# First row tiles transposed before they are scaled, the first scale made in one piece, and a new order, in a decoder layer kernel

## The chip, the core and the metric

The kernel runs on one core of a Trainium2 chip. A core has a matrix engine (TensorE, PE in the profile; its weight loads are shown as PEld), VectorE (DVE), ScalarE (ACT), GpSimd (POOL) and a sync engine (SP) whose queue issues all DMAs here. Matrix products read SBUF and write PSUM, which has 8 banks of 128 x 512 float32. The metric is the device time of one execution in microseconds (us), the median of several runs.

## The reference

One layer, sequence 1024, width 1024, float32. Only the first steps matter here:

```
mod = silu(c) @ w_mod + b_mod            # w_mod: 1024 x 6144; c: one vector
sh1, sc1, g1, sh2, sc2, g2 = split(mod)  # six vectors of 1024
h    = rms_norm(x, norm_mix_w) * (1 + sc1) + sh1
proj = h @ w_in                          # key, z, query, value, lru columns, beta and alpha
```

After that come a gated linear recurrence and a chunked gated delta rule (with a triangular inverse for each chunk), an output projection, a squared-ReLU MLP and a last norm.

## The kernel before

**Products.** A float32 operand is split into two fp32r parts, a high one (`hh`, `wkh`) and a low one (`hl`, `wkl`), and a product is made of three: high by high, high by low, low by high (`mm3`). Transposes, sums and the products for `mod` are plain float32, which the profile records twice for each product.

**Order.** `Recorder` collects every operation of all engines; `schedule` then places them, engine by engine, by a priority, with estimated durations, and `emit` writes them out in that order (line 475 issues them all, so nearly every row of the profile says L475). The priority of an operation is its place in the code at the start (`rec.early`) and its latest start later, plus a number of its own from the table `SHIFTS`. Some operations of PE are only fillers: `WARM` products of a tile of ones with itself (tile `warm`), taken when no other operation of PE is ready in the plan. Once written out, each engine keeps its order: a filler then takes its time whether PE has to wait or not.

**The start** (lines 675 to 1027). The tokens of x are eight row tiles `x0` to `x7`, 128 x 1024. `xnorm(t)` makes the sum of squares on ACT (tile `xj`), its power -1/2 on POOL (`rs`) and scales the tile. Then 128 x 128 blocks are transposed on PE into PSUM, multiplied there by the column `A1 = (1 + sc1) * norm_mix_w` and split: `hh` on ACT, `hl` on DVE. `sh1` is brought in as two extra columns of `h`.

- `scale1(q)` makes `A1` in three pieces (256, 256 and 512 columns of `sc1`). For the first two, PE multiplies `cact` = silu(c) by the weights (`sc_r`, a row of 256 sums in 8 products), DVE copies the row, and one-column products turn it into columns (`sc_c`). For the third, ACT and DVE sum weights times `cact` (`sc_acc`), and 8 one-column products add up the partitions.
- `xquarter` transposes and scales blocks of two row tiles, `xhalf` of four.
- `Key.first` makes the first key products, of the first 512 tokens, four heads of one PSUM bank each (`k_p`): of the first two blocks of `h` in two halves of 256 tokens, of the others in 512. `splitk` splits the key weights `wk`.
- `Key.second` follows with tokens 512 to 767 and the rest; between them stand `ab_third` (tile `ab`, the beta and alpha columns) and the sum for `sh1` (`sh_acc` on ACT and DVE, `sh_c` on PE). The z, query, value and lru projections, the delta rule and the MLP come later.

Of the kernel before, what the change touches and what calls it, by code (L numbers as in the profile page):

```python
# [47 lines left out]
FILL, WARM, AB_DUR, GATE_DUR, L1_DUR, L2_DUR = 1e6, 36, 0.85, 0.89, 0.07, 0.14  # L48
# [7 lines left out]
TABLE = 1.28  # L56
RESERVE = {"b": 11, "ps": 2, "u": 1, "c": 2}
# [67 lines left out]
def dram_box(ap):  # L125
# [7 lines left out]
    'c-p;NXLuFWy8hOhGzcXW30?5es~}a1VCWn`L7Ef+QBXiQqI8rhND~wk2pttfX;OtylwL!ZlF%U}p``8X?Cd@Bo_FWo`{zE-?0Y9a&g99HWY2uF*80l(z'  # L133
    '3-YyCKjQ)H9^YC<D}|VGGY*hW-70qr9Q?AX(@e>h5af*8-~|Y5>aZ0yoxJ0i^cduPN6rpSjBNAd5(1Om6!GE4E{o$gxKWg(p;|MU+VDvb&nP&hCi8+I4'
    'dC`VMEfv<dnpSq$<ycJe&0Fz_ZiO!jmgKpOD(*MWQDnWld_(^PL!tbZa-#5*OgrjMlPIl&na7fFjZi^HPgIq_~=c9x7P&$j%otpYN9TvI&y$)$>v>3d#'
    'JGo*8A8q;1Xm*8Lgh-YP8}ZJ&l3h0Q*4@Yy)5loQ_bXfJ1y`r;EzHFl`8>U_$NdTja}1j!z(OFxRu8I!DrX@BzXhVrT9OMOL-b3`kBq0!y<Fyk+ELYiZ'
    '4dMXxLv&Bk}aCMTl8RKzW*6WTijYxc_%gaFhvV`c-@~%E_EXG5te8~5rCBMYT6x7r{Y>}gBgRLw?>p4;+E7&zjX2=JU*E3(@T=%jfbb_qYC4!IZSlvdh'
    '>*=oh+N<sw_q12W>G-TmYKqZJCAoh!$E)S~JAFPYQbypR>XLa(^_K~{WM*}>N%qTM))tIa^JQ&zL1VV(Mp`Picvj0i>1oB|v@ubwbAPLPsiaKHx`SO<f'
    '~l$r(yWTI$2=k(u@&#*4Yfg@$p{&Oe|kn(ORN;sw6^=2WDSr3^0sQC;*EUfY}}IZ@~u9rPDy9!oHbR>Tj#8GnJ&b5cDdiMhGUF(G}@!OF9^H6OY~(aVH'
    'TB|yzc^u&AQ-u-71HNo<5nCWEryYz{*HXw>D#MW(mo{H@M`Q>;8w^>wZ78k^7*T<=Sk$>rJsztj=-=argi~BHoo`)pk{P|B!jl)j8u$w0FOf9iQFSo#N'  # L140
    '{0nw3$*HxP|7j$3D}1J*-tQ1<Z5f$sCJWA5J=|J(9X=16Y?v%jxy<_bJE_gS?vg0RXe>e}I1ZbryVRPwC#b;9?IO+NK&)}+iw@M0Kdm{&2&{23LkerA~'
    '3z_o2c9+XG_tc%{7mO_53s%xh8n)^NTmgjF@InP9IPtPUa6f@c<4v#P3)Z(J!F=8E$(ae<p@G-=k%6R=>R~ZuIb6YXKj#3XROw+rGsNupYl*SHxY!;Js'
    '%$IVq9{bG8Xz#5k$FqY`-Z~4*J=whC9_vfa{L<aabJcuib;BBtR>x;B-$zIV&tB9=g6CHD)a*}vkyb0SKk`~9d>-F+^Fwp5S;3o$3BIn<TDti9Nk!Q!h'
    'kQ}8Nv39>_KwTCf&JNyef1FR>F-_Zo0)YweYCrSd#k&QtB$L6dfklf=`)dld?;+D`6^2ntDr=Bx?>VDnQINaKYPMa$!zK?ZFaRjl=*nqcf<VMS`5vcoG'
    '5LinVd7Xn)S@r%=?Zb{|(|X6!&n;w*jl<CSJg0mXbPFvQ-)FkZKLZal}~@Es=-F%UUceXAolr5h<pj2?qE+!{1oVue);2id2TYC10~DM_3oo6#Kb?z39'
    '(*j<5z`Ju$Gg<2(Z`dP^z_%VCaPTxv)e*&rq^V>9+)CARaoCAf<G@&XY=>q-)-6LFd-@~L#x*Ht&2f^)b)q<KwJtcohX8j9)C%!tx0f{tKIP?_MH##E!'
    'RJmNhHvs*cxpBB?BgW6ECMB4H1lknkJ`BI`d*9;8c+=t3Xk|0%;KRHY2^Lm&Lmt^AB7L}@Is~}xpO34Wr%EV1;vw9|dq?_)m8mJ|BfQ9O?{Hb>;7kZ(B'
    ')RT*hb_sbRk1<6JQ%`j<Jx*;=f66G;S-$dj7I`E)6r`NQt2?M6qok9RmJcPbZlvz0@oEe^<tepC-J+j9(@W)`)|}^JW36m4MoV>Lw!W;B*l$DCdexY0V'
    '6|GH_Nz9sOA0Yl=HNB?fqt&VDr?Glwv}gaqbnm)i;MeMmr-T)MD>eYL9h|b>)M7?mpLjuXr$4`NKuFMSfi=D926CDP-co{G*C|^Lw4#x#zpBC{EM0?(R'
    '!tERi4W+sbG8}Kk7>Ck}LFVwNR((TPjSKlZL^IBsOTU5h;DygHz$pi*WfyF00#8ovVC?ZTL~9NfIVXwA|!pZ%Q25LSH#76J(_>B|D4~avjr*`sxie&)6'  # L150
    'bfBP=LH#mG@9p`z3>M2c6>!&hpW+)&HaTzNyF2FVR1qphrAt++8n*X6p0%XV3<pX!Y|EGR)&Qe}-As=EG3n(8m4r!18}SP9kSEblW?&d~SEINJ^?PU`d'
    'LVzMpg_@^9Oggdr4fv24JY_cY&$7ANF)1#_m3kwa&FE*lsW6L1r+<)a9TXc|Ygc1MhIksHMY;k(zacr>^Q`l47%)T;2t_TU@x7*M5C7rQP=g&o~Y(<p4'
    'B2!gIc9xMcpP!VGNGamjfqPkfA3L7oImZ@_WCyO{37LIw)Req(3nj$^iyb0S!iZI^abJ8qUqK3!U*5wja*-bBgM#uAqS@18_}44+e^d^FJ3Er_7VVrKB'
    '^+CHlWW*1UD#9h61!_-ri?^!nZ-{^N&y+piVc(P`YzTHmx3i95q7<*s(gr+cd0oRT3(!l+bS#f(NsQ_R#+nk(Nrx*sPs`w*}LM%k<K#%Dv~X|qG}swuv'
    'PM-H7hO=<<u=>z4eY<)T{L_j8nDsr|Os$rK-tyYLFU6wiC)O@&tl6;lV}bmm+%3RcR`kv+AqQsdK6hXA#UkQQ7gzhcUj+Yxh;h7T~O>;UiT@%1d?i4l^'
    'bXz50#3Pgb-_g|jP$>9V?uYN2;Zf378u^x%riNH%?NLA6vPrL;QC?w`r;&Ft8#c+WBX{)4kmQXyjKJW^LLkT<m(?bQ(~>U1QtpRSPY2+kEFUMA%nJI1*'
# [72 lines left out]
class Recorder:  # L229
# [64 lines left out]
    def schedule(self):  # L294
# [40 lines left out]
        while done < len(ops):  # L335
# [115 lines left out]
            for j in op.succs:  # L451
# [4 lines left out]
                if kind and o.eng == "PE" and not o.bb:  # L456
                    r += SLACK_TINY if o.tiny and op.eng == "DVE" else SLACK
# [128 lines left out]
def hybrid_body(ctx, tc, x, c, norm_mix_w, norm_mlp_w, w_mod, b_mod, w_in,  # L586
# [202 lines left out]
    for a in range(4):  # L789
        load_sc1(2, a)  # L790
# [188 lines left out]
    for k in (2, 3):  # L979
        xhalf(0, k)  # L980
# [942 lines left out]
```

## Time and profile before

| | |
|---|---|
| median of 3 runs | 1150.64 us (1147.06 to 1154.63) |
| profiled execution: its time | 1149.7 us |
| its span, first to last instruction | 1147.8 us |
| PE busy | 1135.8 us of it |
| mean granted clock of PE | 0.996 |
| first key product starts | 20.89 us |
| first `ab` product starts | 75.67 us |

The profile was taken on one execution. Rows of a timeline give start, length, engine, operation, the tile written and the tiles read, and how often the operation follows itself; in brackets stands how long the engine was idle before, and what ended that. PE's rows overlap, since a product's end lies behind the start of the next; what one takes of PE is read from start to start. The clock of PE is 1.00 or 0.50 at any moment; a value between is a mean over a stretch.

### The profile page before, as it was taken

The page shows a single profiled execution, that of the slowest core. Times are in us where ns is not written, and L with a number is a line of the kernel's source. Part 1 is how long each engine was busy: PE and PEld are TensorE (multiplying, and loading weights), DVE is VectorE, ACT ScalarE, POOL GpSimd, SP SyncE. Part 2 cuts the span into 40 slices and gives each one's busy share as a digit, 9 for nine tenths or more (in the row PEclk, how much of TensorE's full clock was granted, in tenths as well). Part 3 has the DMA queues.
Part 4 walks back from the last instruction along what each step waited for, and adds up shares of the span by engine and source line. Part 5 has one row for each costly group of instructions (what it writes and reads, how often), then busy time and mean ns, then how long its engine had stood idle before and what let it go on. Part 6 is the DMA issues. An engine that isn't in the chain of part 4 may idle for free.

```text
span 1147.8 us, 16549 instructions
## 1 busy us (share of the span) xinstructions
PE 1135.8 (99%) x6288; PEld 971.7 (85%) x6288; DVE 823.0 (72%) x1143; ACT 611.0 (53%) x961; POOL 274.8 (24%) x161
## 2 busy tenths in 40 slices
PE   8999999999999999999999999999999999999997
PEld 5889998999999987888888888887888888888886
DVE  3559898688888869679767677576874485774673
ACT  4535815454567895577645454556744343452362
POOL 1101100021211334300003211323241085743130
PEclk9999999999999999999999999999999999999999
DMA  9504933447526345241368857877999766774631
GB/s 344 192 19 136 368 102 112 129 129 245 190 71 202 130 147 182 84 156 56 136 231 266 290 205 251 272 256 241 351 390 401 285 223 218 267 284 163 238 110 74
DMA packets 126256, 233.75 MB, mean 204 GB/s; under 512 B 10785, under 2 KB 49886, under 8 KB 126178
## 3 DMA queue, kind: packets, MB, share of 16 engines
q1 hardware_dynamic: 126178, 232.71, 58.6%
q8 instruction: 49, 0.80, 0.3%
q14 instruction: 29, 0.24, 0.1%
HBM read 173.93 MB, written 58.74 MB: 203 GB/s over the span
## 4 chain that ended last, share of the span: by engine, by line
PE 83%; DVE 7%; ACT 6%; issue 2%; DMA 1%; POOL 0%; SPq 0%; POOLq 0%; DVEq 0%; ACTq 0%
PE dn L475 27%; PE upx L475 16%; PE upz L475 8%; PE k_p L475 4%; PE wl L475 4%; PE upy L475 4%; PE v_p L475 3%; PE q_p L475 3%; PE lx_p L475 2%; DVE xr L475 2%; PE ch L475 1%; PE cho L475 1%; ACT ta L475 1%; DVE xx L475 1%; DVE ftmp L475 1%
## 5 line engine op out<-in xcount | busy, mean ns | idle before, releaser
L475 PE MATMUL upx<-h2h,U 128*128 128x512 f32 x512 | 167.8, 394 | 0.0
L475 POOL TENSOR_TENSOR wd<-wd,wd 128x512 f32<-128x512 f32 x32 | 53.2, 1664 | 262.0 <-DMA wd<-in_w_down_dram 173.9
L475 PEld LDWEIGHTS upx<-h2h,U 128*128 128x128 f32 x512 | 96.1, 188 | 22.7
L475 DVE TENSOR_TENSOR U<-wu,U 128x512 fp32r<-128x512 f32 x112 | 84.5, 771 | 24.5 <-ACT U L475 23.8
L475 PE MATMUL upx<-h2l,U 128*128 128x512 f32 x256 | 100.8, 394 | 0.0
L475 ACT ACTIVATE act<-act 128x512 f32<-128x512 f32 x112 | 69.2, 631 | 39.6 <-DVE act L475 38.4
L475 PE MATMUL upz<-h2h,U 128*128 128x512 f32 x256 | 85.0, 394 | 0.0
L475 ACT CAST U<-wu 128x512 fp32r<-128x512 f32 x112 | 66.5, 616 | 25.0 <-DVE wu L475 14.3
L475 PEld LDWEIGHTS upz<-h2h,U 128*128 128x128 f32 x256 | 48.1, 188 | 11.6 <-issue 0.2
L475 PEld LDWEIGHTS upx<-h2l,U 128*128 128x128 f32 x256 | 48.1, 188 | 11.3
L475 DVE TENSOR_TENSOR act<-upz,ek 128x512 f32<-128x512 f32 x32 | 22.0, 688 | 44.5 <-PE upz L475 40.1
L475 PE MATMUL upz<-h2l,U 128*128 128x512 f32 x128 | 50.4, 394 | 0.0
L475 ACT COPY ek<-upx 128x512 f32<-128x512 f32 x48 | 27.7, 582 | 31.1 <-PE upx L475 30.9
L475 PE MATMUL upy<-h2h,U 128*128 128x512 f32 x128 | 42.9, 395 | 0.0
L475 DVE TENSOR_TENSOR wu<-wu,wu 128x512 f32<-128x512 f32 x48 | 38.2, 802 | 0.2
L475 POOL TENSOR_TENSOR xb<-xb,keep 128x512 f32<-128x512 f32 x8 | 13.9, 1745 | 81.9 <-DVE keep L475 81.9
L475 PE MATMUL q_p<-hl,q_wh 128*128 128x342 f32 x96 | 32.4, 337 | 0.0
L475 PE MATMUL q_p<-hh,q_wl 128*128 128x342 f32 x96 | 32.3, 336 | 0.0
L475 PE MATMUL v_p<-hl,v_wh 128*128 128x342 f32 x96 | 31.7, 330 | 0.0
L475 PE MATMUL q_p<-hh,q_wh 128*128 128x342 f32 x96 | 31.6, 329 | 0.0
L475 PE MATMUL lx_p<-hl,lx_wh 128*128 128x342 f32 x96 | 31.6, 329 | 0.0
L475 PE MATMUL ly_p<-hh,ly_wh 128*128 128x342 f32 x96 | 31.5, 328 | 0.0
(587 smaller groups left out, 3576.9 us busy)
## 6 DMA issues: line engine op xcount, KB each, us to landing
L<-aod SPq DMA_DIRECT2D x56, 512.0 KB, 6.7
R<-in_w_down_dram SPq DMA_DIRECT2D x40, 512.0 KB, 4.9
wu<-in_w_up_dram SPq DMA_DIRECT2D x32, 512.0 KB, 4.6
aod<-as SPq DMA_DIRECT2D x64, 256.0 KB, 4.6
wd<-in_w_down_dram SPq DMA_DIRECT2D x32, 512.0 KB, 4.6
aod<-act SPq DMA_DIRECT2D x48, 256.0 KB, 3.7
x<-in_x_dram SPq DMA_DIRECT2D x16, 512.0 KB, 4.2
sc_w<-in_w_mod_dram SPq DMA_DIRECT2D x16, 512.0 KB, 8.7
```

The source lines that it names most:

```text
L475: op.fn(*[res(v) for v in op.a], **{n: res(v) for n, v in op.k.items()})
```

## The change

- Each of the eight loads of `sc1` brings all 1024 columns for one block k of `c`, where it brought 256 columns for four blocks or 512 for two. x0 to x3 are asked for ahead of them.
- `xraw(k)` transposes block k of the four scaled row tiles into one PSUM bank, and ACT and DVE in turns copy it out unscaled, into `xr`. `xscale(k)` later makes `hh` and `hl` from that copy in SBUF. `xquarter` is gone; `xhalf` serves the second half of the tokens as before.
- `scale1` runs once. Blocks 0 to 2 are summed on ACT and DVE over all 1024 columns (`sc_acc`), blocks 3 to 5 on PE as a row (`sc_r`, two banks of 512), blocks 6 and 7 go straight to columns by one-column products with `cact`. The row of `b_mod` is added by one product too. All of it adds up in one PSUM tile `sc_c`, and one DVE instruction makes `A1`.
- `Key.first` is called for 512 tokens throughout: 96 products of 512 columns in place of 72 of 512 and 48 of 256.
- `WARM` is 60 in place of 36, the table `SHIFTS` has new numbers, and in the plan a filler no longer keeps a distance from the filler ahead of it.

```
-FILL, WARM, AB_DUR, GATE_DUR, L1_DUR, L2_DUR = 1e6, 36, 0.85, 0.89, 0.07, 0.14
+FILL, WARM, AB_DUR, GATE_DUR, L1_DUR, L2_DUR = 1e6, 60, 0.85, 0.89, 0.07, 0.14
+SC_V, SC_R = 3, 6
 _SHIFTS = (
-    'c-p;NXLuFWy8hOhGzcXW30?5es~}a1VCWn`L7Ef+QBXiQqI8rhND~wk2pttfX;OtylwL!ZlF%U}p``8X?Cd@Bo_FWo`{zE-?0Y9a&g99HWY2uF*80l(z'
...
-                if kind and o.eng == "PE" and not o.bb:
+                if kind and o.eng == "PE" and not o.bb and not (op.eng == "PE" and o.bias == FILL):
...
-    load_x(0)
-    load_sc1(0, 0)
-    load_x(1)
-    load_sc1(0, 1)
+    load_x(0, 1, 2, 3)
+    for k in range(6):
+        load_mod(1, "sc1", k, sc1_w)
...
     load_wk(0)
-    load_x(2, 3)
-    load_sc1(1, 0)
-    load_sc1(1, 1)
+    for k in range(6, NK):
+        load_mod(1, "sc1", k, sc1_w)
     load_wk(1)
-    for a in range(4):
-        load_sc1(2, a)
...
+    xr = [big(f"xr{q}") for q in range(4)]
+
+    def xraw(k):
+        px = ps(f"xTr{k}")
+        for j in range(4):
+            tr(px[:, j * P:(j + 1) * P], xt[j][:, k * P:(k + 1) * P], ident)
+        (A.copy if k % 2 else V.tensor_copy)(xr[k // 2][:, halves[k % 2]], px)
+
+    def xscale(k):
+        a, b = hT[k]
+        s, r, sc = halves[0], xr[k // 2][:, halves[k % 2]], A1[:, k:k + 1]
+        A.activation(a[:, s], r, AF.Identity, scale=sc)
+        V.scalar_tensor_tensor(out=b[:, s], in0=r, scalar=sc, in1=a[:, s].bitcast(F32), op0=ALU.mult, op1=ALU.subtract)
+
+    def scale1():
+        pc, pr, row = ps("sc1_c"), [ps(f"sc1_r{i}") for i in range(2)], big("sc1_row")[0:1, :]
+        acc = big("sc1_acc")
+        for k in range(SC_V):
+            macc(acc, sc1_w[k], k)
+        for k in range(SC_V, SC_R):
+            for i, h in enumerate(halves):
+                mm(pr[i][0:1, :], cact[:, k:k + 1], sc1_w[k][:, h], k == SC_V, k == SC_R - 1)
+        A.copy(row[:, halves[0]], pr[0][0:1, :])
+        A.copy(row[:, halves[1]], pr[1][0:1, :])
+
+        def cols_(w, r, first, last):
+            for j in range(NK):
+                mm(pc[:, j:j + 1], w[:, j * P:(j + 1) * P], r, first and j == 0, last, skip_group_check=True)
+        cols_(acc, ones[:, 0:1], True, False)
+        mm(pc[:, 0:NK], rows2, ident[0:64, 8:16], False, False, skip_group_check=True)
+        cols_(sc1_w[NK - 2], cact[:, NK - 2:NK - 1], False, False)
+        cols_(row, ones[0:1, 0:1], False, False)
+        cols_(sc1_w[NK - 1], cact[:, NK - 1:NK], False, True)
+        V.scalar_tensor_tensor(out=A1, in0=pc[:, 0:NK], scalar=1.0, in1=bcol[:, 48:56], op0=ALU.add, op1=ALU.mult)
...
-    xnorm(0)
-    xnorm(1)
-    scale1(0)
+    for t in range(4):
+        xnorm(t)
+    for k in range(NK):
+        xraw(k)
+    scale1()
     splitk(0, V, halves_[0])
-    xquarter(0, 0)
     splitk(0, V, halves_[1])
+    for k in range(2):
+        xscale(k)
     for h in range(NH):
-        projs[h].first(0, 0, 256)
...
+        projs[h].first(0, 0, 512)
+    for q in (1, 2, 3):
         splitk(q, V)
         for k in (2 * q, 2 * q + 1):
-            xhalf(0, k)
+            xscale(k)
         for h in range(NH):
             projs[h].first(q, 0, 512)
```

What moves on PE shows at the place where the last columns of the scale are made. Before, the last two pieces of it stood between fillers, with key products of the first two blocks already done ahead of them (`k_p`) and the transposes of the next blocks (`xTp`) behind:

```order
L475 MATMUL k_p_267<-hh_249,wkl_216 128x256
L475 MATMUL warm_125<-ones 128x128
L475 MATMUL k_p_257<-hh_249,wkl_216 128x256
L475 MATMUL warm_125<-ones 128x128
L475 MATMUL sc_c_361<-ones,sc_row_356 128x1 x2
L475 MATMUL warm_125<-ones 128x128
L475 MATMUL sc_c_370<-ones,sc_acc_315 128x1 x4
L475 MATMUL sc_c_370<-ones,sc_acc_306 128x1 x4
L475 MATMUL warm_125<-ones 128x128 x2
L475 MATMUL xTp_0_389<-ident,x_134 128x128
```

In the changed kernel the same place on PE has the columns from blocks 6 and 7 (`sc_w_216`, `sc_w_223`), those from the row (`sc_row`), the last transposes (`xTr`), six fillers, and then the first key product:

```order
L477 MATMUL sc_c<-ones,sc_row 128x1 x4
L477 MATMUL sc_c<-cact,sc_w_216 128x1
L477 MATMUL sc_c<-cact,sc_w_223 128x1
L477 MATMUL sc_c<-ones,sc_row 128x1
L477 MATMUL sc_c<-cact,sc_w_223 128x1
L477 MATMUL sc_c<-ones,sc_row 128x1
L477 MATMUL sc_c<-cact,sc_w_223 128x1 x5
L477 MATMUL xTr_298<-ident,x_110 128x128
L477 MATMUL sc_c<-cact,sc_w_223 128x1
L477 MATMUL xTr_298<-ident,x_116 128x128
L477 MATMUL warm_126<-ones 128x128 x6
L477 MATMUL k_p_364<-hh_352,wkh_289 128x512
```

So every key product now stands behind all of the scale's columns on PE, where all key products of the first two blocks stood ahead of the columns of the last two pieces.

The second place is further down on PE, where the sums of the decay (`gcs`, made from `graw`, the end of a chain of small DVE steps) stand. Before, they were between z projections:

```order
L475 MATMUL z_p_1115<-hh_409,z_wl 128x342
L475 MATMUL z_p_1115<-hh_437,z_wh 128x342
L475 MATMUL gcs<-graw,ones 128x32
L475 MATMUL gcs<-graw,triu 128x32
L475 MATMUL z_p_1115<-hl_449,z_wh 128x342
```

Now they stand among the key products of the last tokens, with fillers around them:

```order
L477 MATMUL k_p_946<-hl_463,wkh_387 128x258
L477 MATMUL k_p_946<-hh_446,wkl_413 128x258
L477 MATMUL warm_126<-ones 128x128 x7
L477 MATMUL gcs<-graw,triu 128x32
L477 MATMUL gcs<-graw,ones 128x32
L477 MATMUL warm_126<-ones 128x128 x3
L477 MATMUL k_p_1058<-hh_352,wkh_289 128x258
```

The 60 fillers of the changed kernel stand on PE in four groups: 31 ahead of the first row sum, 6 ahead of the first key product, 13 among the transposes of x4 to x7 and just behind them, and these 10.

More of the change, by code (lines that the diff above doesn't have):

```diff
@@ new lines @@
+    'f2_&_|;A-^gz)L-URJsW#eO;p$GBt=ZAi>;ZJ@i?{!IHR205;7_0-)1A<Mj4;s_pE)GC|As0{ye!Xv&^*IS-zeA0<(=Ymt8q0GRx&|l<uB*k6)_g7f7p'
+    'u0eBzha3ud@&maKJJh`5WdHb>!X8+~=I6osRzMyR0E^kK8&b*zTJ9#R<M_!-&#`ztkp0~PpME*E$sOPA+vbSb#iQHrP`|^k7j?TO5ZTsk(+@|@ha%Oqs'
+    'Wo}_Yfi`cNQJ9QM3X<eombbXj?@h-2{0)V_dnV?6;7uuLTv#seUg4O+TyIkDW?z~&Mrt6YAX%mt?)Dz?UCmo-Zoo0$8)|0ZN~!E`qCD~;=Bm>E0<6Vy8'
+    '7xnmO?+SKI==PjsnX<}xXe13DCsf}XI-Q9EsT@y#vHSY%8>4AggPMxHc2l$riQEW#?$h-x`!ERflii7xCzrg$9P^HG`>I?9LIOE#$19m1ueBkdp$0+zO'
+    '=wW{|d>KG13(GrGj3irm1b%h1>dwe?6vRkh+OZ%Fqu&*66kVpA02w>T5MYmzLhTpZTKe3g$?(EYNEuN~egz3{%Oc=5%wP>5;AeasGwo8L4en!_#Pn4lW'
@@ new lines @@
+    ';(<fhrme^9!rJo%To#ylV!bpnQ>I~wbr(#<ti&o`>7Y$F?6wJW5Lao%-S-@#A1qiPnqCFF_Fj%uE(u5J}FS&h+s@j0f3%nYgLN;gi3&%7=#=n<|0V?K7'
+    'uGv;C(hM{gq88Z@t<!eN$cE(_%EZQRrm-I||5sfgOGXvVIGJ39BFJZWZXtY!xs)~3=;P4va*rJi?)Z#bC7SA~z)&KP>p-Q6V|N7J;^N{bd%$5zZ&9_?~'
+    '!%8zpZuzdu247QI<nJT*%qQdxbTBtEo<5K(`fqeZ4YiVaP!Ii40@r0fZp$Q<h<2)(-l7KRM2ytqFc^QTOZZ6s(dQ&jCZUro=7`paMqPh>^S=DxPx0500'
+    'luq+Riv32&TL5ctu`CVOxbG=*Uw_BSxde}In~5WmM#7fsEBG<gd_e2m~IxsB>!HyhxJm@m}C?h$r6V+T*i<3Rpd#b^u%VAGq1@Y|1SQk8^_v4Ca5S$lH'
+    'KOF%;W7c7j01=ha|$WS6|~g#$gjis@+(i_Ms#mVI;o8UKy{RLcCh6q7k8&s~Ge{qI<pjefKt3EK=lE#JO@@?PQCL#~XMNuc;=OXbv`AaN(h}mB-vOUF&'
@@ L199 @@
+    '2wyNXr0+CJt?GApZ7+Z5`mUGgNZOUWW|k*36KgT0?F!e1MlW1dukrwH#r`>C661o+3_Mc}(psH|RQt#h6eL+Ry~XpY{2Jt3#;!`eaVjI!zna{|iCT5`}'
+    'S5|1>T@foTIdRgZiDu-%)l79y^#P{kBaifdsM6R=!`JYW(OJSW`0q6C#H~YFFR=um_c--6NYch$kG9!qpwO`}0D8t`jYO>=oKZbww49vxQY7@CkoKBGh'
+    'r0AB!_kCQw7tu~<pf3ifVX{-+QT^aNKTpXky1Y8&`%A^>0>}1c)i;Px%W%f*q`YYD_(j$Py-fAx9OnB*sCC5n#(1d+FT;)?PHic|-?-(=0Ss2F{F7Cts'
+    ')76XFYES@N&'
 )
@@ L765, in load_x @@
             SP.dma_start(out=xt[t], in_=xs[t])
-    def load_sc1(q, a):
-        n = 256 if q < 2 else 512
-        sc1_w[q, a] = w = v3(big(f"sc1_w{q}{a}"), n)
-        m = 1024 // n
-        SP.dma_start(out=w, in_=wm_p[:, m * a:m * a + m, D + q * 256:D + q * 256 + n])
     def load_wk(q):
@@ L920, in xhalf @@
                                op0=ALU.mult, op1=ALU.subtract)
-    def xquarter(q, k0):
-        for i in range(2):
-            px = ps(f"xTq{k0}_{q}{i}")
-            for j in range(2):
-                tr(px[:, j * P:(j + 1) * P], xt[2 * q + j][:, (k0 + i) * P:(k0 + i + 1) * P], ident)
-            a, b = hT[k0 + i]
-            s, sc = slice(q * 256, q * 256 + 256), A1[:, k0 + i:k0 + i + 1]
-            A.activation(a[:, s], px[:, 0:256], AF.Identity, scale=sc)
-            V.scalar_tensor_tensor(out=b[:, s], in0=px[:, 0:256], scalar=sc, in1=a[:, s].bitcast(F32),
-                                   op0=ALU.mult, op1=ALU.subtract)
@@ L933, in scale1 @@
-    def scale1(q):
-        n = 2 if q < 2 else 4
-        ks = slice(2 * q, 2 * q + n)
-        pc = ps(f"sc1_c{q}")
-        w = n * P
-        m = 1024 // w
-        if q < 2:
-            pr, row = ps(f"sc1_r{q}"), big(f"sc1_row{q}")[0:1, 0:w]
-            for k in range(NK):
-                mm(pr[0:1, 0:w], cact[:, k:k + 1], sc1_w[q, k // 4][:, k % 4, :], k == 0, k == NK - 1)
-            V.tensor_copy(row, pr[0:1, 0:w])
-            for j in range(n):
-                mm(pc[:, j:j + 1], row[:, j * P:(j + 1) * P], ones[0:1, 0:1])
-        for a in range(0 if q == 2 else 2, 2):
-            acc = big(f"sc1_acc{q}{a}")[:, 0:w]
-            for k in range(4):
-                wt, c = sc1_w[q, (4 * a + k) // m][:, (4 * a + k) % m, :], cact[:, 4 * a + k:4 * a + k + 1]
-                if k == 0:
-                    A.mul(acc, wt, c)
-                else:
-                    V.scalar_tensor_tensor(out=acc, in0=wt, scalar=c, in1=acc, op0=ALU.mult, op1=ALU.add)
-            for j in range(n):
-                mm(pc[:, j:j + 1], acc[:, j * P:(j + 1) * P], ones[:, 0:1], a == 0 and j == 0, a == 1, skip_group_check=True)
-        V.scalar_tensor_tensor(out=A1[:, ks], in0=bcol[:, 8 + ks.start:8 + ks.stop], scalar=1.0, in1=pc[:, 0:n],
-                               op0=ALU.add, op1=ALU.add)
-        V.tensor_tensor(out=A1[:, ks], in0=A1[:, ks], in1=bcol[:, 48 + ks.start:48 + ks.stop], op=ALU.mult)
@@ L963, in hybrid_body @@
     V.tensor_copy(bcol, pt[:, 0:64])
-    xnorm(0)
-    xnorm(1)
-    scale1(0)
+    for t in range(4):
[3 more added lines that the diff above has]
+    scale1()
     splitk(0, V, halves_[0])
-    xquarter(0, 0)
     splitk(0, V, halves_[1])
+    for k in range(2):
+        xscale(k)
     for h in range(NH):
-        projs[h].first(0, 0, 256)
-    for t in range(2, 4):
-        xnorm(t)
-    xquarter(1, 0)
-    scale1(1)
-    for h in range(NH):
-        projs[h].first(0, 256, 512)
-    splitk(1, V)
-    for k in (2, 3):
-        xhalf(0, k)
-    for h in range(NH):
-        projs[h].first(1, 0, 512)
-    scale1(2)
-    for q in (2, 3):
+        projs[h].first(0, 0, 512)
+    for q in (1, 2, 3):
         splitk(q, V)
         for k in (2 * q, 2 * q + 1):
-            xhalf(0, k)
+            xscale(k)
         for h in range(NH):
```

118 lines of the change are left out of this document (53 added, 65 removed).

## The prediction

> **What bounds the kernel now.** The page comes first, then PE's waits.
>
> ```profile
> span 1147.8 us, 16549 instructions
> ...
> PE 1135.8 (99%) x6288; PEld 971.7 (85%) x6288; DVE 823.0 (72%) x1143; ACT 611.0 (53%) x961; POOL 274.8 (24%) x161
> ...
> PE warm L475 <- DVE ones L475: 2.3, 1, 2.3
> PE sh_c L475 <- DVE sh_acc L475: 0.9, 1, 0.9
> PE crow_ps L475 <- DMA crow<-in_c_dram: 0.9, 1, 0.9
> PE kk L475 <- DVE k3T L475: 0.5, 1, 0.5
> ```
>
> PE is busy for all but 12 us, and its listed waits behind the start are under 3 us. Time can only come from what PE executes: fillers, stretches at half clock, and how late the first useful product starts. A busy PE isn't always a useful one, so I look at its clock and DMA by stretches next.
>
> ```profile
> 8.00:20.00 12.00, 11.83 (x50) 5.75 (x50) 3.11 (x9) 5.62 (x9) 1.11 (x2) 1.00 1.04 397
> 34.00:36.00 2.00, 2.00 (x20) 1.99 (x19) 1.49 (x3) 0.00 (x0) 0.00 (x0) 1.00 1.03 410
> 36.00:38.00 2.00, 2.00 (x14) 2.00 (x15) 1.49 (x4) 0.00 (x0) 1.02 (x1) 0.70 1.03 410
> 38.00:40.00 2.00, 2.00 (x11) 2.00 (x10) 0.07 (x2) 0.76 (x2) 0.44 (x1) 0.50 1.03 395
> 40.00:44.00 4.00, 4.00 (x25) 3.29 (x24) 2.41 (x6) 4.00 (x7) 1.10 (x2) 0.97 0.24 89
> 180.00:220.00 40.00, 39.88 (x485) 36.15 (x484) 28.82 (x37) 17.46 (x26) 2.37 (x1) 0.96 0.45 139
> 220.00:1147.00 927.00, 919.97 (x4561) 779.15 (x4559) 668.04 (x820) 500.81 (x759) 255.22 (x136) 1.00 0.61 210
> ```
>
> The columns are the stretch, its length, busy time of PE, PEld, DVE, ACT, POOL, PE's clock, the DMA share and GB/s. The clock fell at about 36.8 ((1 - 0.70) / 0.5 x 2 = 1.2 us at half before 38) and was back at 40.2, a spell of 3.4 us; 180 to 220 holds another (0.04 / 0.5 x 40 = 3.2 us, as rounded). From 220 on PE has nothing to lose. So the change acts on the first 76 us, and its order on what lies up to 220. The chain of waits and the timeline of PE give what each kind of product takes of PE there.
>
> ```profile
> 20.89 0.73 PE L475 MATMUL k_p<-hh,wkh 128*128 128x256 f32 x4
> 75.67 0.32 PE L475 MATMUL ab<-hh,wab 128*16 128x342 f32 x1
> ...
> 32.29 0.52 PE sc_r L475 x2
> 33.25 0.22 PE warm L475 x2
> 33.81 0.53 PE sc_c L475 x4
> 34.76 1.68 PE sc_c L475 x16
> 37.07 2.35 PE xTp L475 x11
> 47.57 5.11 PE k_p L475 x22
> 60.58 1.85 PE xTp L475 x17
> 62.44 0.07 PE rows_ps L475
> 63.40 1.68 PE sh_c L475 x16
> 65.08 10.76 PE k_p L475 x90
> ```
>
> Per product that is 0.52 us for a row sum of 256, 0.22 for a filler, 1.68 / 8 = 0.21 for a one-column product (two records each), 1.85 / 17 = 0.109 for a transpose, 5.11 / 22 = 0.232 for a key product of 512 columns, 10.76 / 90 = 0.120 for one of 256. At half clock a transpose took 2.35 / 11 = 0.214, twice as much. My mark is the first `ab` product at 75.67: from there on both kernels have the same products, only in another order and with 10 fillers more in the new one.
>
> **The change part by part.**
>
> *Up to the first row sum.* PE has 31 fillers and three transposes there. If the clock rises after one spell of 3.4 us from the first filler on, at 5.7 to 9, some 12 of them run at half rate (0.43) and 19 at 0.22: 2.3 + 5.2 + 4.2 + 0.3 = 12.0. What feeds PE there is due earlier:
>
> ```profile
> 4.39 1.06 ACT L475 ACTIVATE xj<-x 128x1024 f32<-128x1024 f32 x1 [2.39 <-DMA x<-in_x_dram]
> 16.29 1.06 ACT L475 ACTIVATE xj<-x 128x1024 f32<-128x1024 f32 x1 [0.88 <-DMA x<-in_x_dram]
> 49.39 1.16 ACT L475 ACTIVATE sh_acc<-sh_w,cact 128x1024 f32<-128x1024 f32 x1
> 50.59 3.93 DVE L475 SCALAR_TENSOR_TENSOR sh_acc<-sh_w,cact,sh_acc 128x1024 f32<-128x1024 f32 x3 [0.21 <-ACT sh_acc L475]
> 39.24 0.69 ACT L475 ACTIVATE hh<-xTp,A 128x512 fp32r<-128x512 f32 x1 [7.15 <-PE xTp L475]
> 19.75 0.16 DVE L475 SCALAR_TENSOR_TENSOR A<-bcol,sc_c 128x2 f32<-128x2 f32 x1 [0.60 <-PE sc_c L475]
> 39.96 0.75 DVE L475 SCALAR_TENSOR_TENSOR hl<-xTp,A,hh 128x512 fp32r<-128x512 f32 x1 [1.93 <-ACT hh L475]
> 43.94 1.22 DVE L475 TENSOR_TENSOR wkl<-wk,wkh 128x1024 fp32r<-128x1024 f32 x1
> ```
>
> Before, x3 had 4.75 MB landed up to its end and was in use at 16.3; at 0.397 MB/us, with the first tile in use at 4.4, a new tile of 0.52 MB lands every 1.3 us: x3 at 9, the second tile of `sc1` (the first that PE takes) at 11.6, the fourth at 14.3, the sixth at 17, the eighth at 21. SP's other loads stand behind these and keep their bytes. If the fillers stayed at half rate to the end, 31 x 0.43 + 2.3 + 0.3 = 16: up to +4.
>
> *Row sums, transposes, columns.* A sum of 512 columns is 2 x 0.43 + 0.09 = 0.94 (two passes of 0.21 in 0.52 for 256). 6 x 0.94 = 5.6; 29 transposes x 0.109 = 3.2; 33 products of one or eight columns x 0.21 = 6.9; 0.1 for the transposed rows. The columns begin when 22 of the transposes are through, at 12.0 + 5.6 + 2.4 = 20.0, and would end at 27.8. The eighth tile, in use at 21, no longer sets the end: PE does. `sc_acc` is covered: its last tile lands at 15.6, two DVE steps of 3.93 / 3 = 1.31 end it at 18.2, needed at 20.0. Copies into `xr` (0.7 each, four on DVE, four on ACT) run under PE's sums; uncovered, the last two would add 1.4.
>
> *The clock.* In the 3.4 us before it fell at 36.8, one-column products took 0.53 + 1.68 = 2.2 us. Here they take nearly all of 20.0 to 27.8, so it falls between 22.2 and 25.6, by the phase of the spells; I take 23.9. Do such products get slower at half clock? Their weight loads set their pace:
>
> ```profile
> L475 PEld LDWEIGHTS xTq<-ident,x x8: 137/140/183, 7.2 to 23.4; 128*128 128x128 f32 x8
> L475 PEld LDWEIGHTS sc_r<-sc_w,cact x32: 79/80/82, 9.3 to 32.2; 128*1 128x1 f32 x32
> L475 PEld LDWEIGHTS sc_c<-ones,sc_acc x16: 192/192/192, 34.5 to 36.2; 128*128 128x128 f32 x16
> ```
>
> A load of one column takes 80 ns at any time; of what 128 columns add, a transpose's load goes from 60 to 103 at the slow start. So I double: 3.9 us left become 7.6, the columns end at 31.5, six fillers of 0.43 take until 34.1 (they cover `A1` at 0.16 and the first two `hh` at 0.69 each), and the key products run at half rate until a busy spell is over, 0 to 3.4 us, which costs 0.85 in the mean. The wait that the change adds is that of `A1` for all 33 columns; behind it on DVE stand a copy into `xr`, half a `wkl` and four `hl`, for which the first key products wait, and all of PE's work behind these. As if started at 35.0; the phase makes it 33.3 to 36.7.
>
> *Key products to `ab`.* 96 x 0.232 = 22.3, 32 transposes 3.5, 13 fillers 2.9, 96 x 0.120 = 11.5, `sh_c` 1.7, 0.1: 42.0. Per pair of blocks DVE gives 2 x 0.75 for `hl` and 1.22 for `wkl`, 2.7 us for 24 products that take 5.6, so DVE isn't late. `ab` comes at 77.0, 1.3 later than before. That the work itself got shorter (no `k_p` of 256, six sums in place of 16) is in these sums already; before, 20.89 to 75.67 was 54.8 us with the sums and half a scale inside.
>
> *Behind it.* The 10 fillers around `gcs` are worth 2.2 in full, or 0 where PE had to wait for `graw` anyway; I take 2.2, since the listed waits show almost none there. Short products of the inverse cost PE a change each way:
>
> ```profile
> 186.07 1.23 PE L653 MATMUL iw<-aw,LT 64*64 64x64 f32 x18
> 187.29 0.46 PE L475 MATMUL qk<-q0T,kTl 128*128 128x128 f32 x2
> 187.68 0.33 PE L653 MATMUL iw<-aw,LT 64*64 64x64 f32 x2
> 187.93 0.71 PE L475 MATMUL qk<-q0T,kTl 128*128 128x128 f32 x4
> ```
>
> A lone pair took 0.25 from start to start, in the run of 18 it is 1.22 / 9 = 0.14: 0.11 for a change. Runs of `it`, `iy`, `iw`, `iz` go from 23 to 17: -0.7. The half-clock spell within 180 to 220 cost 1.7; the new order packs `iy` in one run and may or may not have one: -0.85 in the mean, 0 to -1.7. In all 2.2 - 0.7 - 0.85 = +0.65, bounds -2.4 to +2.2.
>
> Sum: 1.3 + 0.65 = +1.95 on the span of 1147.8, 1149.75; the profiled execution took 1149.7, 1.9 over its span, which gives 1151.65, say 1151.6. That execution lies 0.9 under the median of 1150.64.
>
> **The rivals.** *Not slowed columns (faster).* If the clock holds, columns end at 27.8, `A1` and two `hh` make the first key product 29.4, and its low part (behind a copy and a split on DVE) costs some 0.7: 30.1 + 42.0 = 72.1, -3.6; with -0.2 behind it (2.2 - 0.7 - 1.7, as no spell would come there either), 1149.7 - 3.8 = 1145.9. Against it: the row of 36 to 38. The Trainium skill, page "TensorE: Matmul & The Clock Gate", section "HAM oscillation — how this bites in real kernels", has the clock fall over gaps in which PE idles longer than about 3.4 us. By that rule a run of products without a gap would hold the clock and this rival would be the result; the trace differs, since the clock fell here behind a run of one-column products in which PE had no gap.
>
> *Key products in spurts (slower).* Where a key product waits for `hl` or `wkl`, spells are never busy enough and the half clock stays through the first key products: 22.3 more for all, 1174. [...]
>
> *The new order waits.* PE's order between 76 and 220 is new at many places, and before lost next to nothing to waits there. Two or three waits like the largest above (0.9) and one more spell at half clock (1.7) make 1156.
>
> *The early rate doesn't come.* Fillers at half rate or loads a few us later move all behind them: +4, 1155.6.
>
> **How the numbers follow.** Forecast 0.58 (own range 1148 to 1155, from the phase, the inverse and `gcs`); held clock 0.20; order waits 0.11; early rate 0.07; spurts 0.04. The likeliest is 1151.6. The range of 1144.5 to 1158 takes in all but the spurts and the tails. About 1% (11.5 us) is what a measurement of this kernel tells from no change, its three runs lie 7.6 apart. Faster by over 1% needs 1139: no case gets there, 0.02 for what I don't see. Slower by over 1% needs 1162: the spurts, and some waits on top of an early loss: 0.06. Within: 0.92.
>
> **What would show it.** The clock row between 20 and 36 should have a spell or two at 0.50; `sc_c` products from about 20 to 31, at 0.21 and then about 0.4; the first `k_p` near 34; `ab` near 77; `gcs` with PE idle or fillers ahead of it. `ab` at 72 to 73 with the clock at 1.00 means the first rival. Row sums that start at 14 or later mean the early one. Wrong altogether if PE is idle for more than some 5 us between 40 and 220.

## The result, and the profile after

The new kernel took 1161.6 us in the median of five runs (1158.75 to 1162.92; a sixth, at 5734, was disturbed and is left out), the kernel before 1151.9 in six runs on the same chip. The ratio is 1.008, with a 95% interval of 1.0051 to 1.0109. So the change made the kernel slower, by 0.8%: within the 1% that the prediction called no change, but 10 us where 1 was forecast, and above its range. The profiled execution took 1162.92 us, the longest of the five.

First the page and PE's waits, as before (for a wait: total, times, longest, us):

```profile
span 1160.4 us, 16663 instructions
...
PE 1146.4 (99%) x6334; PEld 983.3 (85%) x6334; DVE 838.8 (72%) x1134; ACT 613.6 (53%) x964; POOL 271.6 (23%) x161
```

```profile
PE warm L477 <- DVE ones L477: 2.3, 1, 2.3
PE wg L477 <- POOL gcl L477: 1.8, 2, 1.1
PE upx L477 <- ACT U L477: 1.3, 1, 1.3
PE q_p L477 <- issue: 1.1, 1, 1.1
PE oT L477 <- DVE nv L477: 0.6, 1, 0.6
```

The span is 12.6 us longer, and PE is as busy as before: 99%. Three waits for other engines are new, on `gcl`, on `U` and on `nv`, all far behind the start; for the idle 1.1 ahead of `q_p`, at 191.6, the profile shows no cause. The table by stretches shows the rest (length, busy time of PE, PEld, DVE, ACT, POOL, PE's clock, DMA share, GB/s):

```profile
20.00:23.40 3.40, 3.40 (x25) 2.73 (x24) 0.69 (x1) 1.68 (x3) 0.00 (x0) 1.00 1.04 402
23.40:37.00 13.60, 13.60 (x61) 13.42 (x61) 2.84 (x6) 3.47 (x6) 0.00 (x0) 0.50 1.01 373
37.00:43.00 6.00, 6.00 (x22) 4.87 (x21) 5.69 (x8) 6.00 (x11) 1.12 (x2) 0.71 0.50 176
...
415.00:440.00 25.00, 23.18 (x106) 18.68 (x105) 23.84 (x22) 16.17 (x23) 10.19 (x6) 0.93 0.79 274
440.00:475.00 35.00, 34.78 (x153) 27.58 (x153) 22.47 (x26) 20.76 (x28) 16.66 (x8) 0.95 0.18 60
620.00:640.00 20.00, 18.73 (x80) 14.59 (x79) 14.01 (x18) 9.02 (x16) 4.99 (x3) 1.00 0.71 228
```

PE had no idle time from 23.4 to 43, yet its clock stood at half for all of 23.4 to 37 and for (1 - 0.71) / 0.5 x 6 = 3.5 us more. Between 415 and 440 it lost 1.8 us to waiting and (1 - 0.93) / 0.5 x 25 = 3.5 us ran at half clock, a spell of the same length followed before 475, and at 620 to 640 another 1.3 us were idle. The timeline of PE puts places to it:

```profile
11.91 1.88 PE L477 MATMUL sc_r<-sc_w,cact 128*1 128x512 f32 x4
...
20.28 1.95 PE L477 MATMUL sc_c<-ones,sc_acc 128*128 128x1 f32 x16
...
23.43 1.86 PE L477 MATMUL sc_c<-cact,sc_w 128*128 128x1 f32 x8
...
31.97 2.30 PE L477 MATMUL sc_c<-cact,sc_w 128*128 128x1 f32 x10
...
34.91 2.77 PE L477 MATMUL warm<-ones 128*128 128x128 f32 x12
37.33 1.63 PE L477 MATMUL k_p<-hh,wkh 128*128 128x512 f32 x3
...
80.86 0.32 PE L477 MATMUL ab<-hh,wab 128*16 128x342 f32 x1
...
420.68 0.40 PE L477 MATMUL wg<-wo4h,gch 128*128 128x512 f32 x1
...
423.81 0.49 PE L477 MATMUL wg<-wo6h,gcl 128*128 128x512 f32 x1 [1.11 <-POOL gcl L477]
...
475.14 0.39 PE L477 MATMUL wl<-wo0h,lch 128*128 128x512 f32 x1
```

The same marks in the kernel before, beside 75.67 for `ab`:

```profile
416.09 0.39 PE L475 MATMUL wg<-wo4h,gch 128*128 128x512 f32 x1
...
465.14 0.40 PE L475 MATMUL wl<-wo0h,lch 128*128 128x512 f32 x1
```

`ab` is 5.2 later than before, the first `wg` (output projection of the delta rule) 4.6, the first `wl` 10.0. From `wl` to the first `upx` nothing is added; the last `upx` starts 12.2 later and the end of the span comes 12.6 later. So 5.2 were lost in the start, 0.6 won from there to the first `wg`, 5.4 lost in the stage of `wg`, 2.1 in the products with `w_up`, and 0.4 behind them. The first is four times what was forecast there, and the losses in the stages of `wg` and `w_up` lie where the forecast saw nothing to lose.

### The profile page after: what moved, and what is told of

The parts are those of the page before. It is cut to its first block, busy times and chain, and to the rows that moved or that the text cites. A ratio compares the mean times of both kernels' runs of the same rounds, so it can differ in the third digit from the quotient of the medians.

```text
span 1160.4 us, 16663 instructions
## 1 busy us (share of the span) xinstructions
PE 1146.4 (99%) x6334; PEld 983.3 (85%) x6334; DVE 838.8 (72%) x1134; ACT 613.6 (53%) x964; POOL 271.6 (23%) x161
## 4 chain that ended last, share of the span: by engine, by line
PE 92%; issue 3%; POOL 2%; DVE 2%; ACT 1%; POOLq 0%; ACTq 0%; DVEq 0%
PE dn L477 26%; PE upx L477 15%; PE upz L477 7%; PE k_p L477 4%; PE q_p L477 4%; PE z_p L477 4%; PE wl L477 4%; PE v_p L477 4%; PE upy L477 4%; PE lx_p L477 3%; PE ly_p L477 2%; PE wg L477 2%; PE ch L477 2%; PE warm L477 1%; PE sc_c L477 1%
## 5 line engine op out<-in xcount | busy, mean ns | idle before, releaser
L477 POOL TENSOR_TENSOR wd<-wd,wd 128x512 f32<-128x512 f32 x32 | 50.7, 1587 | 285.5 <-DMA wd<-in_w_down_dram 174.3
L477 PE MATMUL upz<-h2l,U 128*128 128x512 f32 x128 | 50.5, 394 | 0.0
L477 ACT ACTIVATE vn<-ch,bcoef 128x128 f32<-128x128 f32 x32 | 11.8, 367 | 43.9 <-PE ch L477 43.6
L477 PE MATMUL q_p<-hh,q_wh 128*128 128x342 f32 x96 | 31.4, 327 | 1.1 <-issue 1.1
L477 PE MATMUL v_p<-hh,v_wh 128*128 128x342 f32 x96 | 31.7, 330 | 0.0
L477 PE MATMUL q_p<-hh,q_wl 128*128 128x342 f32 x96 | 31.6, 329 | 0.0
```

Source lines behind the costliest of these rows:

```text
L477: op.fn(*[res(v) for v in op.a], **{n: res(v) for n, v in op.k.items()})
```

## The experiments

Two theories were set up. **Columns:** the run of one-column products is what lowers the clock and holds it down, and that is the loss of the start. **Order:** the losses behind 400 come from the new order. Its rival: whatever starts 5 us late meets such losses by chance of the clock and the loads. To try orders, the operations were written out in a list that is made of pieces of the two kernels' own orders, in place of the planner's:

```
-        for i in self.schedule():
+        for i in self.fixed():
```

`fixed` returns that list, and each engine takes its operations in its order. With the new kernel's own list the program has the same instructions on the same buffers.

| kernel | median us | ratio to before | 95% | `ab` at | `wg` stage | `upx` stage |
|---|---|---|---|---|---|---|
| before | 1151.9 | | | 75.7 | 49.1 | 311.4 |
| after | 1161.6 | 1.0080 | 1.0051 to 1.0109 | 80.9 | 54.5 | 313.5 |
| h1 new start, old order | 1162.3 | 1.0093 | 1.0072 to 1.0113 | 80.2 | 49.2 | 311.4 |
| h2 old start, new order | 1158.3 | 1.0074 | 1.0051 to 1.0097 | 75.7 | 51.0 | 313.2 |
| v1 sums for columns | 1155.0 | 1.0038 | 1.0023 to 1.0053 | 75.4 | 53.0 | 313.3 |
| v3 sums, old order | 1156.0 | 1.0047 | 1.0030 to 1.0064 | 76.6 | 49.6 | 311.4 |
| f1 casts earlier | 1156.0 | 1.0053 | 1.0028 to 1.0079 | 80.6 | 50.5 | 311.3 |
| e7 new start, exact old order | 1154.8 | 1.0044 | 1.0025 to 1.0063 | 80.4 | 49.3 | 311.4 |
| e8 no gate fillers | 1156.8 | 1.0055 | 1.0036 to 1.0073 | 80.3 | 51.4 | 313.4 |
| c1 sums and casts | 1150.7 | 1.0007 | 0.9993 to 1.0022 | 75.4 | 50.6 | 311.3 |
| g1 c1 and start | 1148.7 | 0.9988 | 0.9973 to 1.0002 | 74.2 | 50.5 | 311.2 |
| g2 g1, no gate fillers | 1148.7 | 0.9990 | 0.9979 to 1.0000 | 74.2 | 50.6 | 311.5 |
| g3 after, again | 1161.2 | 1.0100 | 1.0069 to 1.0132 | 80.5 | 51.4 | 313.3 |
| g4 g1, low parts first | 1147.4 | 0.9979 | 0.9969 to 0.9988 | 74.4 | 49.0 | 312.4 |

The stages are read from each profile: from the first `wg` to the first `wl`, and from the first `upx` to the last. Ratios are to runs of the kernel before on the same chip, which had medians of 1149.9 to 1151.9.

**Sums for columns (v1).** The row sums take two tiles more; their columns go.

```
-SC_V, SC_R = 3, 6
+SC_V, SC_R = 3, 8
...
-        cols_(sc1_w[NK - 2], cact[:, NK - 2:NK - 1], False, False)
-        cols_(row, ones[0:1, 0:1], False, False)
-        cols_(sc1_w[NK - 1], cact[:, NK - 1:NK], False, True)
+        cols_(row, ones[0:1, 0:1], False, True)
```

Two things moved with it in the order: on ACT a cast `wkh` and a copy into `xr` come earlier, and three of the six fillers ahead of the first key product stand ahead of the last columns.

> The new kernel with the sixteen one-column products of the last two tiles of the scale made four row sums of 512 columns (equal time at full clock, 16 x 0.226 = 3.6 against 4 x 0.94 = 3.8); seventeen column products are left, in three short runs. Theory 'columns' (a run of one-column products lowers the clock and holds it low): no half-clock spell between 20 and 40, the columns end near 30, first key product near 31, ab at 72 to 74 in place of 80.9, time 1152 to 1156. Rival 'loads' (the scale is late for its tiles whatever PE does): ab at 78 to 81, time 1159 to 1163.

PE's timeline in v1, and the stretch that stood at 0.50 in the new kernel:

```profile
21.30 1.95 PE L580 MATMUL sc_c<-ones,sc_acc 128*128 128x1 f32 x16
...
24.45 2.73 PE L580 MATMUL sc_r<-sc_w,cact 128*1 128x512 f32 x6
27.11 1.05 PE L580 MATMUL sc_c<-ones,sc_row 1*128 1x1 f32 x8
...
30.08 1.05 PE L580 MATMUL sc_c<-ones,sc_row 1*128 1x1 f32 x8
...
32.81 0.96 PE L580 MATMUL k_p<-hh,wkh 128*128 128x512 f32 x3 [0.82 <-ACT hh L580]
...
75.39 0.32 PE L580 MATMUL ab<-hh,wab 128*16 128x342 f32 x1
```

```profile
23.40:37.00 13.60, 12.65 (x62) 7.76 (x60) 7.23 (x12) 8.78 (x13) 0.36 (x1) 1.00 1.03 371
```

The clock held, and `ab` came 5.5 earlier though the first sum came 1.0 later. The sixteen products taken out are worth what the four put in are, at full clock; what went is the half clock. `ab` missed the 72 to 74 by 1.4: the later first sum, and 0.8 of waiting for `hh`, which ACT began at 31.4, as soon as it had `A1`. "Columns" holds for the 16 products taken out; the 17 that are left can still cost a spell, as v3 shows.

**Two splices.** The first cut lies behind the fillers at the gate sums, some 100 us in (not 190, as its text says).

> The new kernel up to the ten fillers around the gate sums (some 190 us into the span: no later), then every engine in the order of the kernel before; same work, only the order behind the start is put back. Theory 'order' (the 7 us lost behind the start come from the new order): the waits on gcl and U and the half-clock spells at 426 and 467 go, the start keeps its 5.2 late and the gate its 1: span 1153.5 to 1156, time 1155 to 1158. Rival 'late start' (whatever starts 5 us late meets the waits and spells by the phase of the clock and the loads): they stay in some form, time 1160 to 1163.

> The mirror image: the kernel before up to the same place, then every engine in the order of the new kernel. Theory 'order': waits on gcl (1.8) and U (1.3) and one or two spells of 1.7 appear behind an undisturbed start, less 1.6 won in the inverse: 1154 to 1158. Rival 'late start': no such waits, and the 1.6 are won: 1149 to 1152.

Neither came out cleanly. By its time h1 (1162.3) fits the rival, but the waits on `gcl` and `U` are gone; h2 (1158.3) lies 0.3 above what "order" gave. Waits of h2:

```profile
PE gcs L580 <- DVE ssk L580: 2.5, 1, 2.5
...
PE wg L580 <- POOL gcl L580: 1.7, 2, 0.9
PE gT L580 <- DVE gcs L580: 1.3, 1, 1.3
...
PE upx L580 <- ACT U L580: 0.6, 1, 0.6
```

Behind an undisturbed start the new order has the wait on `gcl` and one on `U`, and its `wg` and `upx` stages are 1.9 and 1.8 longer than before; h1, with the old order there, has neither. That speaks for "order". But each splice also lost at its own cut, where the two orders had done different sets of operations. h2 waited 3.8 us for the gate sums there. In h1 the first stretch below lies behind the cut; the second is in the lru projections, far from it, and its cause isn't shown. PE lost 1.9 and 0.9 to waits and its clock was down for (1 - 0.89) / 0.5 x 15 = 3.3 and (1 - 0.72) / 0.5 x 12 = 6.7 us.

```profile
110.00:125.00 15.00, 13.15 (x78) 12.42 (x77) 13.87 (x21) 7.93 (x14) 2.58 (x1) 0.89 0.53 150
340.00:352.00 12.00, 11.07 (x60) 9.47 (x60) 5.88 (x11) 7.16 (x11) 1.71 (x2) 0.72 0.00 1
```

**Sums and old order (v3)** was cut at the same place.

> Both edits: row sums in place of the sixteen column products, and the order of the kernel before behind the start. If both theories hold the gains add: 1161.7 less 8 (start) less 6 to 7 (order) = 1146.5 to 1149, under the 1151.9 of the kernel before. If only 'columns' holds: 1152 to 1156. If only 'order' holds: 1155 to 1158.

It missed, at 1156.0, which either theory alone would have given. By its stages the order's gain is there; some 3.5 us went behind the cut, as in h1: waits on `gT` and `z_st` of 1.0, 0.5 and 0.3, and 1.7 in a half-clock spell. And its start, though the same as in v1, had a half-clock spell of 3.4 us from 24.8 on: `ab` came at 76.6 and not at 75.4. A clean cut was wanted.

**New start, exact old order (e7).**

> The new start, cut at a place where both kernels have done the same set of operations (some 85 us in, behind the first products of ab), then exactly the order of the kernel before, without the ten fillers. Theory 'order': behind the start nothing is lost that the kernel before doesn't lose; its time plus the 5 us of the start, 1154 to 1157. Rival 'late start': the waits and half-clock spells of the earlier splice (113, 343) come again, 1159 to 1163.

1154.8, as "order" had it: `ab` 4.7 later than before and the end 4.1 later, both stages within 0.2 of the kernel before, no half-clock spell between the start and the last 4 us. In this execution a late start alone costs what the start costs. Three of e7's ten took 1157.1 to 1160.8, at mean clocks of 0.985 to 0.989 where the other seven had 0.992 and 0.993; where these three lost it, no profile shows.

**Casts earlier (f1).** What in the order makes PE wait? One row for each kernel lists the casts `gch` on ACT (count, shortest/median/longest ns, first and last start), first before, then after:

```profile
L475 ACT CAST gch<-gcm x8: 604/610/622, 388.5 to 420.6; 128x512 fp32r<-128x512 f32 x8
```

```profile
L477 ACT CAST gch<-gcm x8: 603/616/622, 415.1 to 422.5; 128x512 fp32r<-128x512 f32 x8
```

POOL makes four low parts `gcl` from them; its last two, before and after:

```profile
413.06 2.79 POOL L475 TENSOR_TENSOR gcl<-gcm,gch 128x512 fp32r<-128x512 f32 x2 [3.66 <-ACT gch L475]
```

```profile
421.16 4.27 POOL L477 TENSOR_TENSOR gcl<-gcm,gch 128x512 fp32r<-128x512 f32 x2 [2.00 <-ACT gch L477]
```

Before, the casts began 28 us ahead of the first `wg`, and the last `gcl` was done at 415.9, 0.2 ahead of it. In the new order they begin 5.6 ahead, and the last `gcl` is done at 425.4, 4.8 behind it: PE waits for these two. The wait on `U` stands on ACT, too:

```profile
633.19 1.30 ACT L477 ACTIVATE act<-act 128x512 f32<-128x512 f32 x2 [5.47 <-DVE act L477]
634.40 0.60 ACT L477 CAST U<-wu 128x512 fp32r<-128x512 f32 x1
...
636.07 0.60 ACT L477 CAST U<-wu 128x512 fp32r<-128x512 f32 x1
```

ACT sat 5.5 us ahead of the pair `act` while two casts `U`, which PE needs next, stood behind it. f1 moves four of the eight `gch`, two ahead of the second `tg` and two behind the next `lsq` (and POOL's `gcl` with them), and both `U`; ACT's order at the first and the last place:

```
 ACTIVATE tg<-ly_st 128x1024
+CAST gch<-gcm 128x512
+CAST gch<-gcm 128x512
 ACT_TABLE_LOAD
 ACTIVATE tg<-tg 128x1024
...
 COPY ek<-upx 128x512
+CAST U<-wu 128x512
+CAST U<-wu 128x512
 ACTIVATE act<-act 128x512 x2
-CAST U<-wu 128x512
 ACTIVATE act<-upx 128x512
 ACTIVATE act<-act 128x512
-CAST U<-wu 128x512
```

> The new kernel, with ten operations moved ahead in its order: four casts gch on ACT and their four low parts gcl on POOL, from 415 to 424 up to some 403 to 409, and two casts U on ACT from behind the pair act that waits until 633 for DVE, to ahead of it. Theory 'late casts' (the order puts these casts where PE is already waiting): no wait of PE on gcl and none on U, 1.8 + 1.3 us less, and 1.7 more where the gap at 422 to 426 had halved the clock: 1156.5 to 1159, start unchanged (ab near 81). Rival 'next wait' (something else is as late): waits of the same size on other tiles at the same places, 1160 to 1163.

1156.0, a little below what "late casts" gave. Both waits are gone and no other took their place; the `upx` stage is back at 311.3, and 428 to 453, around the first `wg` at 433.4, shows PE without idle time at full clock (this profile is of the slowest of f1's runs, 1169.0; the second row says why):

```profile
428.00:453.00 25.00, 25.00 (x124) 20.34 (x123) 22.54 (x23) 17.69 (x24) 2.54 (x2) 1.00 0.82 294
...
190.00:225.00 35.00, 34.04 (x197) 28.24 (x196) 14.54 (x21) 9.67 (x15) 2.36 (x1) 0.56 0.26 76
```

In that execution the clock stayed at half for (1 - 0.56) / 0.5 x 35 = 31 us of the triangular inverse, which no other profile here has.

**No gate fillers (e8)**: `WARM` 50, and the order without them.

> The new kernel without its last ten fillers (around the first gcs), all else and all order the same. If they only add: 2.2 less, 1158.5 to 1160. If they stand where PE would wait for ssk and the gate sums anyway (as gcs waited 2.5 and gT 1.3 where the new order ran without them): a wait of about 2 on gcs or gT in their place, 1161 to 1163, and a half-clock spell near 100 can come.

1156.8, lower than either side. Its profile has one wait of 1.2 on `gT` in place of 2.2 us of fillers, 1.0 less, and no half-clock spell between the start and the last 4 us. Whether the spells at 426 and 467 go with the fillers or come by chance, the new kernel itself had to show.

**The new kernel again (g3).**

> The new kernel again, same instructions in the same order, for its spells at 426 and 467. If they come with the waits at their places: again at these places, clock 0.988 to 0.991, 1161 to 1163. If they come by the phase of the clock's windows against the work: other places or none behind the start, the clock up to 0.993, 1157 to 1162.

1161.2 in the median, and this time the profiled execution took 1158.1. The waits on `gcl` (1.8) and in the stage of `w_up` (1.3) are at their places again; the spells at 426 and 467 aren't:

```profile
415.00:440.00 25.00, 23.19 (x111) 18.11 (x110) 23.84 (x22) 17.62 (x24) 9.62 (x5) 1.00 0.80 274
440.00:475.00 35.00, 34.79 (x158) 28.18 (x158) 25.60 (x31) 18.09 (x24) 17.11 (x8) 1.00 0.19 61
```

The stage of `wg` took 51.4 here and 54.5 in the first profile: 3.1 us of those 5.4 are two spells that an execution may have or not, 2.3 are the waits. Most have some: of the eleven executions of the new kernel ten had a mean clock of 0.991 or less, against 0.993 here, and 3.41 us at half are worth 0.0015 of the mean. The span of e8 (1155.0) is 0.9 below this one (1155.9): that is what the fillers cost. But e8's median is 4.3 below this one, and five of its six executions had a clock of 0.993: by the clock, most executions without the fillers had no such spells either. Why is not shown.

**Both together (c1)**, with casts and a low part `wkl` ahead of the copies of the scale row.

> Row sums in place of the sixteen column products, the ten operations moved ahead as in the run of that name, and at the start two casts wkh on ACT and a low part wkl on DVE put ahead of the copies of the scale row, for which the first hh had stood behind 1.6 us of casts. If 'columns' and 'late casts' both hold: 1155.0 less 2 to 4 for gcl and U, less 0.8 for hh: 1150 to 1152.5, level with the kernel before. If only 'columns' holds: 1154 to 1155.

1150.7, level with the kernel before. The gains add; the wait of 0.8 on `hh` stayed, though the casts were out of the way: ACT began `hh` at 31.6, when `A1` came, and made `hh1` ahead of `hh0`.

**Three versions beyond (g1, g2, g4)**: `WARM` 55 (g2: 45), `hh0` ahead of `hh1`, and in g4 DVE's copy into `xr`, half a `wkl` and `hl0` drawn ahead.

> The kernel with sums and casts, with two more edits at the start: the scaling hh0, for which the first key product waits, ahead of hh1 on ACT (the wait of 0.8 on hh), and five fillers fewer ahead of the first row sum (5 x 0.217 = 1.1; the trace of the new kernel had its first sum at 11.9 without a wait). First row sum near 12.0, first key product 31.3, ab 73.7; 1150.7 less 1.7 = 1149.0. If the tiles of the scale aren't there before 13: PE waits at sc_r, 1150 to 1150.7.

> The same without the ten fillers at the gate sums too. By the run without them (a wait of 1.2 on gT in place of 2.2 of fillers): 1.0 less, 1148.0, and 0.2% under the kernel before, if no half-clock spell comes near 100; 1151 or more if the clock halves there, as it did for 6.8 us where the new order ran behind the old start without them.

> The kernel of all edits and the start, with DVE's order around the scale changed: the copy into xr and the half of wkl that stood behind A1 go ahead of it (DVE has nothing to do for 6 us there), and hl0 goes ahead of hl1. The wait of 1.1 on hl goes, ab at 73.1, nothing else changes: 1148.7 less 1.1 = 1147.6, a ratio of 0.997 to 0.998 to the kernel before. If another operand is as late (wkl or the second hh): 1148.5 or more.

g1 took 1148.7 with `ab` at 74.2 and not 73.7, as PE then waited 1.1 for `hl`. g2 gained nothing on it, at 1148.7 as well; the waits on `gT` (1.2) and `U` (0.5) took most of what the fillers had cost. g4 took 1147.4, a ratio of 0.9979 (0.9969 to 0.9988): 0.2% under the kernel before, and 1.2% under the change as it was made. Its wait on `hl` is gone. Its `ab` stands at 74.4, not 73.1, because its profile has a half-clock spell of 3.4 us from 22.9 on, worth 1.7. Its `upx` stage is 1.1 longer than c1's, with a wait of 0.5 on `U`.

## Why the prediction was wrong

- **First row sum, and the work up to `ab`: right.** 11.9 against 12.0; in g3 it was 13.1, so the close match is partly luck. Counted back from `ab` by the 42.0 us of work, the key products began as if at 80.9 - 42.0 = 38.9; the trace has 37.3 and 3.2 us of them at half rate, which is 38.9.
- **"Which costs 0.85 in the mean", "3.9 us left", "the columns end at 31.5": mis-sized.** The clock fell at 23.4, against 23.9. But the columns had begun 0.3 later, took 0.226 and not 0.21 each, and the transposes between the first and the second eight came ahead of them. At the fall 24 products (48 records) and two transposes (one record each, unlike the sums and fillers) were left, 24 x 0.226 + 0.2 = 5.6 at full rate, not 3.9. Doubling was right, they took 34.9 - 23.4 = 11.5 (though 3.9 doubled is 7.8, and 7.6 was put in). Six fillers followed, and the rise came only after a window full of key products. The start lost 5.2, not 1.3: 3.2 of the error are columns and fillers, 0.7 the key products at half rate.
- **The rival of a held clock** was refuted for this kernel, and v1 shows that it is there to be had: its clock held, and `ab` came at 75.4. The Trainium skill, page "TensorE: Matmul & The Clock Gate", section "HAM oscillation — how this bites in real kernels", ties the fall to idle gaps; here the clock stood at 0.50 over 13.60 us in which PE was busy for 13.60. The measurement decides.
- **"The 10 fillers around `gcs` are worth 2.2 in full": too much.** 0.9 to 1.0; the rest hides a wait.
- **The inverse and the order up to 220: in the bounds, with the other sign.** From `ab` to the first `wg` the new kernel won 0.6 (1.4 in g3), where a loss of 0.65 was forecast. 1.7 of it is the spell at 197 in the profile of the kernel before; the new kernel has none there in its two profiles.
- **"From 220 on PE has nothing to lose": the step that failed.** It was read from the order before, in which PE waits for nothing there, and taken over for an order that is new on every engine. The rival of waits from the order had the mechanism, but only between 76 and 220, and with a chance of 0.11. The waits in the stages of `wg` and `upx` cost 2.3 and 1.9 in g3 (51.4 - 49.1, 313.3 - 311.4); h2 shows them with the old start, e7 and f1 show them gone with the old order or ten operations moved. Spells of the half clock added 3.1 on top in the first profile, and come in most executions. The error of the start alone would have left the time at 1151.6 + 3.9 = 1155.5, inside the range.

What stays open: what brings the spells behind 400, and with it some 3.4 us of the medians (4.3 between g3 and e8, of which the fillers are 0.9). The profiles hold one execution each.

## What to carry to other kernels

When an order is new, look at each engine's queue through the whole program, and not at PE's alone near the change: an operand that is done 0.2 us ahead of its stage, as the last `gcl` was, has no room to come later, though no wait shows in the old trace. Work that feeds PE many one-column products should be made of long rows where the cost at full clock is equal. A part of a change that looks neutral by its sum can be undone alone; here the gains of two such edits added up.

## What the runs showed of the hardware

- **The clock fell in a run of one-column products without a gap.** Their weight loads kept PE busy, and still the clock fell and stayed at half for 17 us (23.4 to 40.5). All six profiles with 33 such products (the new kernel, h1, f1, e7, e8, g3) stood at half for four or five windows of 3.41 us there; of the six with 17 (v1, v3, c1, g1, g2, g4), two did for one window (v3, g4) and four not at all. At half clock such a load took 333 ns, against 192 at full:

```profile
L477 PEld LDWEIGHTS sc_c<-ones,sc_acc x32: 186/192/192, 20.3 to 323.3; 128*128 128x128 f32 x32
...
L477 PEld LDWEIGHTS sc_c<-cact,sc_w x32: 285/333/370, 23.4 to 34.4; 128*128 128x128 f32 x32
```

- **Spells lie on a grid of 3.41 us that is placed differently from one execution to the next.** In the new kernel they begin at 23.4, 426.2 and 467.2: 118 and 12 times 3.413 apart. The Trainium skill, page "TensorE: Matmul & The Clock Gate", section "What's actually happening", has a free-running window of 3413 ns; the trace agrees with the length, and the spells of the 14 profiles, modulo 3.413, start between 0.9 and 3.0 us. The place on the grid can decide what a short run of such products costs. The sums for the lru norm (`lrus`, eight one-column products, 1.9 us) lay within one window of the grid in the profiles of the new kernel, v1, f1, c1, g1 and g2, and in each the next window was at half clock (some 1.5 us lost: f1, c1, g1 and g2 take 50.5 or 50.6 in the `wg` stage, the kernel before 49.1). They lay across an edge in those of the kernel before, h1, h2, v3, e8, g3 and g4, and in none of these the clock fell. In e7 they began within 0.02 us of an edge, and it didn't fall. But the place is not all: the sums for `sh1` (`sh_c`, eight such products too) lay within one window in eight profiles (h1, h2, v3, f1, e7, e8, g3, g4), and the clock fell behind none of them. What else counts is open.
- **The half clock once lasted through a stage of short products**: f1's execution with 31 us at half in the inverse took 1169.0, 13 us over its median. One of g3's took 1172.4 at the same mean clock, 0.978; where it lost them no profile shows.
